# Finished byte addresses instead of element offsets in the table that places each matmul's output in PSUM

## The chip, the cores and the metric

The kernel runs on one core of one Trainium2 chip. The metric is the device time of one execution in microseconds (us).

## The reference, cut to what matters

```python
N, E, D = 4096, 262144, 256
def reference(nodes, edges_src, edges_dst, w_msg, w_self):
    self_out = nodes @ w_self
    msg = nodes[edges_src] @ w_msg
    agg = np.zeros((N, D), dtype=np.float32)
    np.add.at(agg, edges_dst, msg)
    return self_out + agg
```

Every edge adds the transformed row of its source node to its destination node.

## The kernel before

The kernel has two phases. First VectorE sorts all edges by (block of 512 destinations, block of 128 sources, destination). Then the chunk loop turns the sorted edges into counts: 128 edges make one chunk, 2048 chunks in all. For each chunk, two one-hot matrices (source within its block of 128, destination within a window of `W` = 96) are multiplied, and the 128x96 product is added into a ring of six banks, as the kernel's parts of 512 columns are called here, in PSUM (the memory that the kernel takes for the results of its matmuls). *Where* in the ring depends on the data, so the offset comes from a table made after the sort, and TensorE reads it into registers.

The table before holds offsets in elements:

```python
    tt(out=dl[:], in0=dl[:], in1=ex[:], op=ALU.subtract)
    tt(out=poff[:], in0=wr[:], in1=dl[:], op=ALU.add)            # element offset in the ring
    nc.scalar.dma_start(pd[0, :].rearrange("(p g) -> p g", g=G16), poff[:])
    nc.scalar.dma_start(poffs[:], pd[0:1, :])
```

One-hots are built on VectorE for 16 chunks at a time (`SL = 16`). The pair "c" is for chunks; the pair "h" is for heads, the 256 matmuls that open a run at a fixed address:

```python
    def onehots(src, rel, tag):
        for nm, val, wid in (("e", src, P), ("d", rel, W)):
            o = ohp.tile([P, SL // 2, wid, 2], BF16, name=nm + "_oh", tag=nm + tag,
                         bufs=8 if tag == "c" else 2)
            tt(out=o[:], in0=val..., in1=jrow..., op=ALU.is_equal)
```

The loop (cut; "run" is one ring bank of 512 columns, some 8 chunks):

```python
        for c in range(NCOL):                                  # 2048 chunks
            ci = c % SL
            if ci == 0:
                e, d = onehots(slo_b[:, sl_], rel_b[:, sl_], "c")
                # ... and now and then heads[nhead] = onehots(hsl, hrel, "h")
            # ... head_mm(r, ...) where run r starts: fixed address
            if c % 8 == 0:
                regs = [nc.tensor.alloc_register(f"po{c}_{i}") for i in range(8)]
                nc.tensor.load(regs, poffs[0:1, c:c + 8])      # 8 offsets, one load
            off = nc.tensor.snap(regs[c % 8], donate=True, min_val=0, max_val=RING * SEGW - W)
            count_mm(ring[:, bass.ds(off, W)], e, d, ci, False)
            # ... evac(run): ScalarE copies a finished bank to SBUF as bf16 ("at")
            # ... apply_run(run): 4 matmuls out_ps += at.T @ Y (Y: the transformed rows, nodes @ w_msg);
            #     at every 32nd run also 8 "self" matmuls (nodes @ w_self)
```

The matmul is given a byte address, so `off` becomes `off * 4 + 0x2000000`: one fused register operation (for the multiply and the add) for each chunk. The trace before holds 2048 of them on TensorE, of 37 ns each. "TensorE's sequencer" (PEq in the profiles) is the name here for what spends its time on such register operations and on the loads of registers.

## Time and profile before

| | before |
|---|---|
| median of the runs | 985.86 us (985.71 to 986.1) |
| sort and set-up, to the first matmul of the loop | 547.4 us |
| chunk loop | 429.5 us, 256 groups of 8 chunks |
| VectorE busy in the loop | 293 us |

The first excerpt is the page's strip of busy tenths, one digit for each fortieth of the span. VectorE fills the first half. In the loop TensorE shows 8 or 9 tenths.

```profile
PE   0033301131111120302011689888898888898896
...
DVE  3999999989999989898995996776766767767740
```

The second is the windows view of the loop: after the stretch and its length come the busy times (and counts) of PE (TensorE's matmuls), PEld (its weight loads), DVE (VectorE), ACT (ScalarE) and POOL (GpSimd), then the granted clock of TensorE, the DMA share and GB/s.

```profile
547.40:976.90 429.50, 382.12 (x3392) 293.56 (x3392) 292.99 (x285) 156.53 (x270) 0.00 (x0) 0.99 0.03 10
```

PE busy for 382 of 429.5 us looks like a full array. It isn't: the records of matmuls overlap (a ring matmul records some 203 ns, and two can start 42 ns apart, as shown below), so PE also looks busy when they start 115 ns apart. The timeline of two groups shows the pace (start, length, engine, line, operation, count, and in brackets the idle time before it with what ended it):

```profile
703.58 1.01 PE L321 MATMUL ring<-d_oh,e_oh 128*128 128x96 bf16 x9 [0.17 <-issue]
703.58 0.79 PEld L321 LDWEIGHTS <-e_oh 128*128 128x128 bf16 x8 [0.35 <-issue]
...
704.42 0.60 PE L363 MATMUL out_ps<-Y,at 128*128 128x256 bf16 x4
704.62 1.23 DVE L305 TENSOR_TENSOR e_oh<-slo_b,jrow 128x2048 bf16<-128x2048 bf16 x1 [1.16 <-PE ring L321]
...
705.20 1.01 PE L321 MATMUL ring<-d_oh,e_oh 128*128 128x96 bf16 x9 [0.17 <-issue]
```

A group of 8 chunks and one head (9 ring matmuls) starts every 1.62 us. VectorE waits 1.16 us for TensorE before it may overwrite a one-hot. TensorE waits for nothing that the profile names ("issue"). Over the whole loop, the view of waits (total us, times, longest) says the same:

```profile
DVE e_oh L305 <- PE ring L321: 110.6, 96, 1.9
PEld L321 <- issue: 98.8, 269, 5.0
PE ring L321 <- issue: 50.0, 242, 4.7
...
PE ring L321 <- DVE d_oh L305: 0.9, 3, 0.6
```

The page leaves register instructions out, but the trace holds a record of each. Here are single records of TensorE (ns from the start of the span, length in ns; weight loads left out), the end of one group and the start of the next:

```
702443   37  register operation (fused: multiply, add)
702530  203  matmul, ring
702558   37  register operation
702572  204  matmul, ring (head, fixed address)
702645  204  matmul, ring
702673   37  register operation
702760  203  matmul, ring
702798  591  load of 8 registers
702802  270  matmul, out_ps          ... and three more
703489   37  register operation
703575  203  matmul, ring
```

Register operations start 115 ns apart (1630 of 2047 gaps are exactly that). The head slips in 42 ns after its neighbour without delaying anything, so the array could go far faster. What fills the 115 ns can't be read from these records: 37 ns are recorded, 78 ns aren't.

### The profile page before, as it was taken

Reading aid. Unit: us, or ns where it says so; the run is one execution under the profiler, and the core shown is the slowest. Engines: PE = TensorE matmul, PEld = TensorE weight load, DVE = VectorE, ACT = ScalarE, POOL = GpSimd, SP = SyncE. Lnnn points to the kernel's source line nnn. Section 1 sums busy time; section 2 is a strip of 40 time slices with the busy share of each in tenths; the row PEclk is TensorE's granted clock in tenths of the full one; section 3 lists DMA queues with packets and bytes.
Section 4 is the critical chain, followed back from the end, with each engine's and each line's share of the span. In section 5 each row is a group of like instructions: output and inputs, shape, how many; then the busy total and the mean of one; then the engine's idle time right before and its main releaser. Section 6 shows DMA issues by size and latency. Waiting matters only on the chain.

```text
span 983.7 us, 11709 instructions
## 1 busy us (share of the span) xinstructions
PE 477.3 (49%) x3730; PEld 349.9 (36%) x3730; DVE 780.3 (79%) x850; ACT 221.1 (22%) x449; POOL 14.2 (1%) x24
## 2 busy tenths in 40 slices
PE   0033301131111120302011689888898888898896
PEld 0000001121111110202011466666666666676664
DVE  3999999989999989898995996776766767767740
ACT  0011101021010110101003133333333333333333
POOL 4000000000000000000000000000000000000000
PEclk9999999756555555555555699999999999999999
DMA  8611100000000000000003000000000000000000
GB/s 228 134 26 27 24 0 0 1 1 0 0 0 0 0 1 0 0 0 0 0 0 93 1 2 23 1 23 1 1 23 2 23 1 23 2 23 1 23 2 24
DMA packets 25217, 18.03 MB, mean 18 GB/s; under 512 B 11557, under 2 KB 24358, under 8 KB 24390
## 3 DMA queue, kind: packets, MB, share of 16 engines
q1 hardware_dynamic: 19862, 11.59, 4.0%
q0 software_dynamic: 4720, 2.49, 1.9%
q10 hardware_dynamic: 578, 3.16, 0.8%
q8 instruction: 39, 0.64, 0.3%
q14 instruction: 18, 0.15, 0.0%
HBM read 10.12 MB, written 7.37 MB: 18 GB/s over the span
## 4 chain that ended last, share of the span: by engine, by line
DVE 48%; PE 43%; issue 6%; DMA 3%; ACT 0%; DVEq 0%; SPq 0%
PE ring L321 25%; PE out_ps L363 11%; DVE XA_85 L572 7%; DVE XA_84 L572 7%; DVE XA_85 L573 7%; DVE XA_84 L573 6%; DVE XB_86 L572 4%; DVE XB_87 L572 4%; DVE XB_87 L573 3%; DVE XB_86 L573 3%; PE tp_sw L533 3%; DMA XB_86<-in_edges_dst_dram 2%; DVE e_oh L305 1%; DVE d_oh L305 1%; DMA fd<-bcol 1%
## 5 line engine op out<-in xcount | busy, mean ns | idle before, releaser
L321 PE MATMUL ring<-d_oh,e_oh 128*128 128x96 bf16 x2304 | 262.8, 206 | 52.1 <-issue 50.0
L321 PEld LDWEIGHTS <-e_oh 128*128 128x128 bf16 x2304 | 202.6, 97 | 128.1 <-issue 98.8
L305 DVE TENSOR_TENSOR e_oh<-slo_b,jrow 128x2048 bf16<-128x2048 bf16 x128 | 156.4, 1222 | 110.6 <-PE ring L321 110.6
L337 ACT CAST at<-ring 128x512 bf16<-128x512 f32 x256 | 149.8, 586 | 284.2 <-PE ring L321 284.2
L363 PE MATMUL out_ps<-Y,at 128*128 128x256 bf16 x1024 | 153.6, 273 | 0.0
L305 DVE TENSOR_TENSOR d_oh<-rel_b,jrow 128x1536 bf16<-128x1536 bf16 x128 | 121.4, 949 | 0.0
L363 PEld LDWEIGHTS <-at 128*128 128x128 bf16 x1024 | 84.7, 97 | 11.5 <-ACT at L337 0.2
L533 PE MATMUL tp_sw<-ident,XA_85 128*128 128x128 f32 x80 | 20.4, 432 | 111.5 <-DVE XA_85 L573 110.8
L182 PE MATMUL y_ps<-wcat,XT 128*128 128x256 bf16 x64 | 25.2, 394 | 97.3 <-DMA XT<-nodes_bf_dram 97.2
L572 DVE TENSOR_TENSOR XA_85<-XA_84 128x1024 f32<-128x1024 f32 x56 | 68.6, 1225 | 2.2
L572 DVE TENSOR_TENSOR XA_84<-XA_85 128x1024 f32<-128x1024 f32 x55 | 67.4, 1225 | 2.2
L573 DVE TENSOR_TENSOR XA_85<-XA_84 128x1024 f32<-128x1024 f32 x56 | 68.2, 1218 | 0.0
L573 DVE TENSOR_TENSOR XA_84<-XA_85 128x1024 f32<-128x1024 f32 x55 | 67.0, 1218 | 0.0
L533 PEld LDWEIGHTS tp_sw<-ident,XA_85 128*128 128x128 f32 x80 | 14.2, 191 | 117.6 <-DVE XA_85 L573 70.0
L533 PE MATMUL tp_sw<-ident,XA_84 128*128 128x128 f32 x64 | 15.8, 430 | 68.9 <-DVE XA_84 L573 68.9
L182 PEld LDWEIGHTS <-XT 128*128 128x128 bf16 x64 | 6.6, 104 | 115.6 <-DMA XT<-nodes_bf_dram 115.6
L524 ACT COPY XB_86<-tp_sw 128x128 f32<-128x128 f32 x40 | 15.0, 375 | 118.0 <-PE tp_sw L533 97.7
L572 DVE TENSOR_TENSOR XB_86<-XB_87 128x1024 f32<-128x1024 f32 x30 | 36.7, 1225 | 1.0
L572 DVE TENSOR_TENSOR XB_87<-XB_86 128x1024 f32<-128x1024 f32 x30 | 36.7, 1225 | 1.0
L533 PEld LDWEIGHTS tp_sw<-ident,XA_84 128*128 128x128 f32 x64 | 11.5, 190 | 73.3 <-DVE XA_84 L573 70.0
L573 DVE TENSOR_TENSOR XB_87<-XB_86 128x1024 f32<-128x1024 f32 x30 | 36.5, 1218 | 0.0
L573 DVE TENSOR_TENSOR XB_86<-XB_87 128x1024 f32<-128x1024 f32 x30 | 36.5, 1218 | 0.0
(477 smaller groups left out, 286.3 us busy)
## 6 DMA issues: line engine op xcount, KB each, us to landing
out_dram<-o_sb SPq DMA_DIRECT2D x16, 256.0 KB, 2.4
XB_86<-in_edges_dst_dram SPq DMA_DIRECT2D x2, 1024.0 KB, 8.4
XB_87<-in_edges_src_dram ACTq DMA_DIRECT2D x2, 1024.0 KB, 8.5
nodes_bf<-in_nodes_dram POOLq DMA_DIRECT2D x1, 2048.0 KB, 19.9
nodes_bf_dram<-nodes_bf SPq DMA_DIRECT2D x1, 2048.0 KB, 8.7
XT<-nodes_bf_dram SPq DMA_TRANSPOSE x64, 2.4
xs_dram<-XA_85 ACTq DMA_DIRECT2D x1, 1024.0 KB
gball<-gd SPq DMA_DIRECT2D x1, 1024.0 KB, 4.7
```

The source lines that it names most:

```text
L182: nc.tensor.matmul(out=y_ps[:], lhsT=XT[:, k, t * P:(t + 1) * P], rhs=wcat[:, 2 + k, :], start=(k == 0), stop=(k == 1),)
L305: tt(out=o[:], in0=val.rearrange("p (g i) -> p g i", i=2).unsqueeze(2).to_broadcast(shp), in1=jrow[:, 0:wid, :].unsqueeze(1).to_broadcast( ...
L321: mm = nc.tensor.matmul(out=ap, lhsT=e[:, ci // 2, :, ci % 2], rhs=d[:, ci // 2, :, ci % 2], start=start, stop=True, skip_group_check=True ...
L337: ins = nc.scalar.copy(out=at[:], in_=ring[:, b:b + SEGW]).ins
L363: nc.tensor.matmul(out=out_ps[:, t, :], lhsT=at[:, t * P:(t + 1) * P], rhs=Y[:, b, :], start=False, stop=(b == T - 1), skip_group_check=True,)
L524: nc.scalar.copy(out=out_ap, in_=in_ap)
L533: nc.tensor.transpose(tp[:], src[:, g * P:(g + 1) * P], ident[:])
L572: nc.vector.tensor_tensor(out=lo_d, in0=lo_s, in1=hi_s, op=ALU.min)
L573: nc.vector.tensor_tensor(out=hi_d, in0=lo_s, in1=hi_s, op=ALU.max)
```

## The change

Its intent: let VectorE put finished byte addresses into the table, once, so that TensorE's sequencer computes nothing for each chunk.

```diff
+PSUM0 = 0x2000000
@@
     tt(out=poff[:], in0=wr[:], in1=dl[:], op=ALU.add)
+    nc.vector.tensor_scalar(
+        out=poff[:], in0=poff[:], scalar1=2, scalar2=PSUM0,
+        op0=ALU.logical_shift_left, op1=ALU.bitwise_or,
+    )
@@
-            off = nc.tensor.snap(
-                regs[c % 8], donate=True, min_val=0, max_val=RING * SEGW - W
-            )
+            addr = nc.tensor.snap(
+                regs[c % 8], donate=True, min_val=PSUM0, max_val=PSUM0 + 4 * (RING * SEGW - W)
+            ).with_bounds(
+                min_val=PSUM0, max_val=PSUM0 + 4 * (RING * SEGW - W),
+                guaranteed_mod_val=0, out_of_modulus=4,
+            )
+            off = (addr - PSUM0) // 4
             count_mm(ring[:, bass.ds(off, W)], e, d, ci, False)
```

The edit tells the compiler that the address is a multiple of 4, so that it may cancel `(addr - PSUM0) // 4` against `* 4 + PSUM0`.

## The prediction

> **What bounds the kernel now.** The span is 983.7 us. Until 547 us VectorE sorts (the page's slices: DVE 9 tenths); the change leaves that alone but for one tiny operation. From 547 to 977 us runs the chunk loop: 256 groups of 8 chunks. The timeline shows each group as 9 ring matmuls in 1.01 us, 4 out matmuls in 0.44 us and some 0.18 us of "issue". PE's busy share there (89%, the windows view) hides that the array is not the limit. The trace's single records of TensorE show it:
> - every chunk has one fused register operation (2048, 37 ns each, not counted by the page); consecutive ones mostly start exactly 115 ns apart;
> - a head matmul with a fixed address falls 42 to 45 ns after its neighbour and costs nothing: both intervals add up to 115 again. So the array could go at about 43 ns; the 115 ns is the sequencer's;
> - once per group, a load of 8 registers takes 590 ns, and the next register operation starts 100 ns later. From a group's last dynamic matmul to the next group's first is 820 ns; the 4 out matmuls hide inside.
>
> 7 x 115 + 820 = 1625 ns; quiet groups measure 1617 to 1635, the mean is 1671. TensorE's sequencer bounds the loop.
>
> **What the change does.** Each register operation multiplies by 4 and adds 0x2000000, where the ring starts. With finished addresses the expression should collapse to the loaded register, so all 2048 vanish. Register loads, matmuls and one-hots stay. Added: one 128x16 VectorE operation (under 0.3 us).
>
> **What it is worth.** At least the recorded 37 ns. [...]
>
> **Next limit.** VectorE's one-hots: saturated, an e/d pair starts every 2.0 us; 144 pairs make 288 us, 1.13 us per group. The new sequencer period is about 1.26 us, so VectorE, 8 buffers ahead, should rarely be waited for, but its idle time nearly vanishes. ScalarE (0.59 us per group) and the array (0.82 us) are no limit.
>
> **Prediction.** 883 us, 8 in 10 within 864 to 906. Faster by over 2%: 0.93; within 2%: 0.06; slower: 0.01.
>
> **What would show it.** No fused register operations in the loop; dynamic matmuls about 64 ns apart (58 to 75); ring x9 in 0.6 us; "issue" before it still near 0.15 us; register load still 590 ns; mean group near 1.26 us, the loop about 323 us; all before 547 us within 1 us of before; VectorE busy near 90% in the loop.
>
> **What would make it wrong.** (1) The expression doesn't collapse: same time. (2) Only the recorded 37 ns are saved: 908 us. (3) A matmul addressed by a register costs more[...]: nearer 905. (4) VectorE or evacuations bind first: the loop stays over 300 us with such waits in the chain. (5) The register load or its gap grows.

Terms of the sum under "What it is worth" are cut, because no trace of this case showed what they rested on. The sum came to 103 us (986 - 103 = 883 us): 104 us for 2048 operations at 51 ns each (my estimate, with a range of 40 to 57 ns), with 1 to 2 us more and small new waits against them. The 64 ns between matmuls (115 - 51) and the 1.26 us of a group (1671 - 8 x 51 ns) follow from the same estimate.

## The result, and the profile after

The changed kernel takes 842.91 us (842.41 to 843.85, 4 runs) against 985.86 us. The ratio is 0.8551, with a 95% interval of 0.8536 to 0.8566. (Ratios in this document are the mean time of a kernel's fast runs over that of the kernel before in the same rounds, so not quite the ratio of the medians.) That is 143 us less, where 103 were predicted; the time lies below the predicted range.

All of it lies in the loop. The first loop matmul starts at 546.9 us (547.4 before); the added VectorE operation takes 153 ns. The loop takes 287.6 us instead of 429.5:

```profile
546.90:834.50 287.60, 242.18 (x3392) 211.46 (x3392) 284.43 (x285) 156.71 (x270) 0.00 (x0) 0.98 0.04 15
```

The busy time of VectorE, 284.43 of 287.60 us, is now 99% of the loop. The strip shows it too:

```profile
PE   0033320111111111111101112088888888888786
...
DVE  3999999999999999999999998599999999999995
```

The trace has no register operation of TensorE in the loop any more. The timeline of a stretch where one-hots lay ready:

```profile
699.76 0.51 PEld L326 LDWEIGHTS <-e_oh 128*128 128x128 bf16 x9
699.87 0.55 PE L326 MATMUL ring<-d_oh,e_oh 128*128 128x96 bf16 x9
700.12 0.94 DVE L310 TENSOR_TENSOR d_oh<-rel_b,jrow 128x1536 bf16<-128x1536 bf16 x1
...
700.26 0.60 PE L368 MATMUL out_ps<-Y,at 128*128 128x256 bf16 x4
...
700.70 0.55 PE L326 MATMUL ring<-d_oh,e_oh 128*128 128x96 bf16 x9
700.99 1.21 DVE L310 TENSOR_TENSOR e_oh<-slo_b,jrow 128x2048 bf16<-128x2048 bf16 x1
```

A group now starts every 0.83 us, and PE has no gap. In the single records the ring matmuls follow each other by 43 to 45 ns. The register load still takes 588 ns, but in this stretch it starts at the fourth or so ring matmul of the group *before* the one that it serves; it has gone behind the array's work.

In most places one-hots are not ready, and then TensorE waits for VectorE:

```profile
690.10 0.94 DVE L310 TENSOR_TENSOR d_oh<-rel_b,jrow 128x1536 bf16<-128x1536 bf16 x1
...
691.09 0.55 PE L326 MATMUL ring<-d_oh,e_oh 128*128 128x96 bf16 x9 [0.37 <-DVE d_oh L310]
...
692.10 0.94 DVE L310 TENSOR_TENSOR d_oh<-rel_b,jrow 128x1536 bf16<-128x1536 bf16 x1
...
693.10 0.55 PE L326 MATMUL ring<-d_oh,e_oh 128*128 128x96 bf16 x9 [0.18 <-DVE d_oh L310]
```

The waits of the loop have turned round. The 110.6 us in which VectorE waited for TensorE are gone from the list, and the weight loads' "issue" has fallen from 98.8 to 43.2 us; new are the waits of matmuls and weight loads for one-hots:

```profile
PEld L326 <- issue: 43.2, 96, 0.8
PE ring L326 <- DVE d_oh L310: 38.4, 88, 1.6
PEld L326 <- DVE e_oh L310: 11.7, 15, 0.9
...
PE ring L326 <- issue: 5.5, 3, 4.6
```

The mean group is 1116 ns (1671 before); 555 ns x 256 groups = 142 us, which is the whole gain. VectorE starts one pair every 2.005 us, and 144 pairs x 2.005 / 256 groups = 1.128 us per group, about 12 ns from the measured mean.

So the new limit is plain. What the trace alone does not say is why the old one gave way so completely. The prediction had the sequencer go on at some 64 ns per chunk.

### The profile page after: what moved, and what is told of

It reads as the page before. It is cut to its first block, busy times and chain, and to the rows that moved or that the text cites. A ratio compares the mean times of both kernels' runs of the same rounds, so it can differ in the third digit from the quotient of the medians.

```text
span 841.4 us, 9662 instructions
## 1 busy us (share of the span) xinstructions
PE 337.7 (40%) x3730; PEld 268.0 (32%) x3730; DVE 772.9 (92%) x851; ACT 221.6 (26%) x449; POOL 15.1 (2%) x24
## 5 line engine op out<-in xcount | busy, mean ns | idle before, releaser
L326 PE MATMUL ring<-d_oh,e_oh 128*128 128x96 bf16 x2304 | 147.5, 208 | 44.6 <-DVE d_oh L310 38.4
L310 DVE TENSOR_TENSOR e_oh<-slo_b,jrow 128x2048 bf16<-128x2048 bf16 x128 | 154.3, 1206 | 0.0
L326 PEld LDWEIGHTS <-e_oh 128*128 128x128 bf16 x2304 | 132.2, 99 | 66.6 <-issue 48.1
L368 PEld LDWEIGHTS <-at 128*128 128x128 bf16 x1024 | 86.5, 97 | 7.4 <-ACT at L342 0.6
L542 PE MATMUL tp_sw<-ident,XA_85 128*128 128x128 f32 x80 | 20.5, 436 | 111.3 <-DVE XA_85 L582 110.6
L542 PEld LDWEIGHTS tp_sw<-ident,XA_85 128*128 128x128 f32 x80 | 14.3, 193 | 117.4 <-DVE XA_85 L582 70.1
L187 ACT CAST Y<-y_ps 128x256 bf16<-128x256 f32 x32 | 11.9, 372 | 96.8 <-PE y_ps L183 96.8
```

Source lines behind the costliest of these rows:

```text
L187: nc.scalar.copy(out=Y[:, t, :], in_=y_ps[:])
L310: tt(out=o[:], in0=val.rearrange("p (g i) -> p g i", i=2).unsqueeze(2).to_broadcast(shp), in1=jrow[:, 0:wid, :].unsqueeze(1).to_broadcast( ...
L326: mm = nc.tensor.matmul(out=ap, lhsT=e[:, ci // 2, :, ci % 2], rhs=d[:, ci // 2, :, ci % 2], start=start, stop=True, skip_group_check=True ...
L368: nc.tensor.matmul(out=out_ps[:, t, :], lhsT=at[:, t * P:(t + 1) * P], rhs=Y[:, b, :], start=False, stop=(b == T - 1), skip_group_check=True,)
L542: nc.tensor.transpose(tp[:], src[:, g * P:(g + 1) * P], ident[:])
```

## The experiments

Two questions: what did the 115 ns per chunk consist of, and what binds now?

Theory P, formed on seeing the result: a register operation has a fixed price of about 115 ns on TensorE's sequencer, of which the trace records 37; a matmul whose address comes from a register costs the sequencer almost nothing. Its rivals are in the expectations: A (the price is the arithmetic), W (the matmul waits for a freshly written register), S (the price is paid for each change between register operation and matmul). The prediction's own split, an estimated 51 ns for the operation and the other 64 of the 115 ns for the matmul, is the fourth.

The OR with 0x2000000 leaves a finished address as it is, so these kernels stay correct.

### One register operation per chunk put back

```diff
+            fin = nc.tensor.alloc_register(f"fin{c}")
+            nc.tensor.reg_alu(fin, regs[c % 8], PSUM0, ALU.bitwise_or)
             addr = nc.tensor.snap(
-                regs[c % 8], donate=True, ...
+                fin, donate=True, ...
```

> After, with one register operation per chunk put back (an OR with 0x2000000, which leaves a finished address as it is); the matmul reads its result. One plain operation instead of the fused multiply and add of before. Theory P (fixed price): a register operation costs TensorE's sequencer about 115 ns[...]: group period back near 1625 to 1670 ns, about 986 us [...]. Rival A (arithmetic): the cost grows with the number of operations fused, so one costs about half: about 57 ns per chunk, loop near the one-hots' limit, 845 to 870 us.

Measured: 980.58 us, ratio to before 0.9954 (0.9926 to 0.9983), correct. The operations record 32 ns (37 for the fused two) and start 112 or 113 ns apart; a quiet group takes 1598 ns. So one OR takes back nearly all that the change had gained (138 of 143 us). Theory A falls: two operations fused cost 115 ns, one costs 112.5.

### The same operation, its result read 8 chunks later

```diff
             if c % 8 == 0 and c + 8 < NCOL:
+                regs = ...                      # one group ahead
+                nc.tensor.load(regs, poffs[0:1, c + 8:c + 16])
+            nxt = nc.tensor.alloc_register(f"fin{c + 8}")
+            nc.tensor.reg_alu(nxt, regs[c % 8], PSUM0, ALU.bitwise_or)
+            fins.append(nxt)
             addr = nc.tensor.snap(
-                regs[c % 8], ...
+                fins[c], ...
```

> The same OR per chunk at the same place in the stream, but its result is read by the matmul 8 chunks later (registers are loaded one group ahead). Theory P (fixed price per register operation, whoever reads it): same as e1, about 986 us, operations 115 ns apart. Rival W (the matmul waits for a register that has just been written): the operations no longer hold anything up, dynamic matmuls go at about 43 to 60 ns, 843 to 850 us.

Measured: 979.99 us, ratio 0.9948 (0.992 to 0.9977), correct; operations again 112 or 113 ns apart. Who reads the result, and when, does not matter: theory W falls.

### The operation on every second chunk

```diff
+            fin = regs[c % 8]
+            if c % 2 == 1:
+                fin = nc.tensor.alloc_register(f"fin{c}")
+                nc.tensor.reg_alu(fin, regs[c % 8], PSUM0, ALU.bitwise_or)
```

> The OR only on odd chunks, 4 per group. Theory P: the sequencer's group is 700 + 4 x 115 = 1160 ns in quiet groups, about 1200 in the mean, a little over the 1125 ns of the one-hots: 855 to 880 us. Were the slow pace a mode of the whole group (any register operation makes all register-addressed matmuls slow), it would stay near 986 us.

Measured: 868.17 us, ratio 0.8813 (0.8788 to 0.8839), correct. A quiet group takes 1137 ns, 461 less than with eight operations: 115 each. The price is paid per operation; it is no mode of the whole group.

### The eight operations of a group in a row

```diff
                 nc.tensor.load(regs, poffs[0:1, c:c + 8])
+                for i in range(8):
+                    nc.tensor.reg_alu(fins[i], regs[i], PSUM0, ALU.bitwise_or)
             addr = nc.tensor.snap(
-                regs[c % 8], ...
+                fins[c % 8], ...
```

> The 8 ORs of a group in a row directly after the register load, then the 8 matmuls. Theory P: 8 x 115 ns in a row, then the matmuls at 43 ns; the sequencer's group is 1620 to 1670 ns as before, about 986 us. Rival S (the unrecorded 78 ns is paid when the stream changes from a register operation to a matmul and back, not per operation): 8 operations follow each other at 40 to 60 ns, plus one change: group about 700 + 450 = 1150 ns, 850 to 870 us.

Measured: 962.83 us, ratio 0.9774 (0.9746 to 0.9803), correct. Between the two expectations, and much nearer to P. The single records (ns, length) show why:

```
701265  592  load of 8 registers
701961   32  register operation
702054   32  register operation      ... eight of them, 92 or 93 ns apart
702609   32  register operation
702669  206  matmul, ring
702711  213  matmul, ring
702761  590  load of 8 registers
```

In a row, with nothing between them, the operations still start 92.5 ns apart while each records 32. So about 60 ns of every operation are its own and unrecorded, and some 20 ns more appear when a matmul stands between two of them. S is right for those 20 ns and wrong for the rest. The parts of a quiet group are 590 (load) + 105 (to the first operation) + 7 x 92.5 + 152 (last operation to next load) = 1494 ns; the median group takes 1537. Without its eight operations the quiet group leaves 1494 - 8 x 92.5 = 754 ns, 56 more than the 698 of the other runs (below). Those 56 ns are paid once per group; for what, no run shows.

### Half of the one-hots, after the change

```diff
             if ci == 0:
-                e, d = onehots(slo_b[:, sl_], rel_b[:, sl_], "c")
+                if (c // SL) % 2 == 0:
+                    e, d = onehots(slo_b[:, sl_], rel_b[:, sl_], "c")
```

> After, with each pair of chunk one-hots built once and used for two blocks of 16 chunks (wrong result on purpose): VectorE's work in the loop falls from 144 pairs to 80, 160 us. Theory D (after is bound by VectorE's one-hots, 2.0 us per pair): the loop shortens to the next limit, the array at 9 x 43 + 4 x 109 = 823 ns per group plus the 8 self matmuls every 32 groups, about 218 us: 775 us (768 to 790). Rival: the after loop is bound by TensorE (its sequencer or the array): no change, 843 us.

Measured: 799.2 us, ratio 0.8099 (0.8064 to 0.8134); the result is wrong on purpose. The direction is as theory D has it: VectorE's busy time falls from 284 to 156 us, and the kernel gets 44 us faster. So VectorE's work does bind the kernel after. The size missed: 799 is above the 768 to 790 expected. Quiet groups have the array's pace (median 830 ns against 823 expected), but the mean is 941. The waits of the loop (window 560 to 770 us) name what is left:

```profile
DVE e_oh L310 <- PE ring L326: 60.9, 13, 5.9
...
PE ring L326 <- issue: 6.6, 13, 1.2
```

The page's groups put all of those 60.9 us before the one-hots of the heads:

```profile
L310 DVE TENSOR_TENSOR e_oh<-hsl,jrow 128x2048 bf16<-128x2048 bf16 x16 | 19.5, 1221 | 60.9 <-PE ring L326 60.9
```

VectorE waits there until TensorE has used an older pair of the heads, for example 3.13 us until the operation that starts at 693.04 us. At 695.32 us TensorE in its turn has waited 0.70 us; the profile calls it "issue", and it ends 0.19 us after the head's one-hots are finished, so it was probably for them. That the two buffers of the heads cause this was not tested.

### Half of the one-hots, before the change

The same edit on the kernel before.

> Before, with the same halving of the one-hots (wrong result on purpose). If before was bound by TensorE's sequencer alone, nothing changes but small waits: 975 to 985 us. If VectorE was part of the limit of before, it falls by 20 us or more.

Measured: 985.42 us, ratio 0.9986 (0.9946 to 1.0026). VectorE has half the work in the loop, and the time stays:

```profile
547.00:977.00 430.00, 383.06 (x3392) 293.81 (x3392) 158.15 (x158) 156.78 (x270) 0.00 (x0) 0.99 0.03 10
```

The mean group takes 1670 ns as before. So VectorE was no part of the limit before. Nor was the array: after the change the same matmuls follow each other by 43 to 45 ns. What is left is TensorE's sequencer.

### The register load twice

```diff
                 nc.tensor.load(regs, poffs[0:1, c:c + 8])
+                regs2 = [nc.tensor.alloc_register(f"pq{c}_{i}") for i in range(8)]
+                nc.tensor.load(regs2, poffs[0:1, c:c + 8])
+                regs = regs[0:4] + regs2[4:8]
```

> After, with the 8 registers of each group loaded by two loads (the first half of the matmuls reads one set, the second half the other). Theory: the sequencer's only remaining cost in after is the load, 590 ns plus about 100 not recorded, 700 ns per group, hidden under the one-hots' 1125 ns. With two, 1380 ns per group come to the front: loop about 355 us, 905 us (890 to 925). Were loads free to overlap with each other, the array or the one-hots, 843 us.

Measured: 931.82 us, ratio 0.9443 (0.9406 to 0.9481), correct. The sequencer binds again:

```profile
PEld L326 <- issue: 148.1, 233, 0.8
PE ring L326 <- issue: 89.4, 208, 0.6
DVE e_oh L310 <- PE ring L326: 63.3, 78, 1.9
```

The median group is 1394 ns (1380 expected). The time is 7 us above the expected range because the mean group is 1465: I had left out the longer groups that the kernel before has as well (1671 in the mean against 1617 to 1635 in quiet ones).

This run also holds the most telling pair of numbers. From the first load of a group to the second, with nothing between them, the median is 688 ns, of which 587 are recorded. From the second load to the next group's first, with 8 register-addressed matmuls, 5 fixed ones and 13 weight loads between, it is 707 ns. So 26 engine instructions add 19 ns to the sequencer's time. A matmul addressed by a register does not cost it the 64 ns that the prediction left for it: eight of those would have added 512 ns.

### A version that goes with the new limit

Since VectorE binds now, larger one-hots should help if part of each of its operations is fixed, as the two sizes suggest (see the expectation; the kernel after measures 1135 and 869 ns from start to start for 2048 and 1536 elements, which leaves an estimated 4 x 869 - 3 x 1135 = 71 ns if the rest grows with the size):

```diff
-SL = 16
+SL = 32
@@
-                bufs=8 if tag == "c" else 2,
+                bufs=4 if tag == "c" else 2,
```

> After, with one-hots built for 32 chunks at a time instead of 16 (4 buffers instead of 8, same values). If VectorE binds the loop and about 65 ns of each of its 288 operations is fixed (1130 and 870 ns from start to start for 2048 and 1536 elements in the same lanes: 0.55 and 0.57 ns per element), half of that, 9 us, falls away, less some 3 us for a later first block and a longer last one: 835 to 839 us, inside 2%. Were TensorE the limit, 843 us or a little more.

Measured: 833.91 us, ratio to before 0.8447 (0.8421 to 0.8474), correct: 1 us below the expected range. A one-hot of twice the size starts its successor after 2202 and 1669 ns, against 2 x 1135 and 2 x 869, so 68 and 69 ns of each operation are fixed (65 expected). It ran again beside the kernel after and a mixed version (blocks of 32, but 16 for the first two, the last two and the heads):

> The kernel after, unchanged, as the measure on this chip for the two below: 842 to 844 us.

> One-hots for 32 chunks at a time, unchanged from c1: 833 to 835 us, 1.1% faster than after.

> As c1, but the first two and the last two blocks, and the heads' one-hots, are of 16 chunks. VectorE's fixed part rises by 1 us for the heads and 0.5 us for the small blocks; the first matmul should come some 3 us earlier than in c1 and the last matmuls some 1.5 us sooner after the last one-hot: 830 to 833 us. If start and tail do not count, 835 us.

On that chip the kernel after took 843.0 us (842.87 to 843.31), blocks of 32 took 833.25 us (832.46 to 835.25), and the mixed version took 835.94 us (835.04 to 837.73), all correct. Blocks of 32 take 1.2% less than the kernel after, and their runs lie clear of its runs; against the mixed version the ranges just overlap. From the heads' one-hots that open the loop (at 544 us) to the end of the last one-hot, VectorE takes 275.3 us with them, 286.7 in the kernel after, and 278.2 in the mixed version. So the mixed version's earlier start did not pay for its smaller operations: that expectation was missed, and only about half of the 2.9 us follows from its ten extra pairs. In the groups of the repeated run, VectorE has no idle time before the one-hots of the chunks:

```profile
L310 DVE TENSOR_TENSOR e_oh<-slo_b,jrow 128x4096 bf16<-128x4096 bf16 x64 | 145.5, 2273 | 0.0
...
L310 DVE TENSOR_TENSOR d_oh<-rel_b,jrow 128x3072 bf16<-128x3072 bf16 x64 | 111.4, 1741 | 0.0
```

## Why the prediction was wrong

- **What bounds before: right.** Halving VectorE's work left before at 985.4 us; putting one OR back per chunk brought after to 980.6 us.
- **What vanishes: right.** All 2048 register operations are gone, and the start of the loop moved by 0.5 us only.
- **What it is worth: this step failed.** The prediction put the operation at 51 ns (40 to 57) of the 115 and left 64 for the matmul. The operation measured 112 to 115 ns between matmuls, more than double. The split was my estimate; no trace showed it. The trace already spoke against it: a head matmul with its weight load cost the 115 ns nothing (it starts 42 to 45 ns after its neighbour, and the operations around it stay 115 ns apart). I took the matmul with a register address for an exception, without saying so. It isn't one: 26 engine instructions, eight of them such matmuls, add 19 ns.
- **The group's sum, corrected.** The sequencer's group is about 698 ns for load and rest, plus 112 to 115 ns for each register operation: 1598 - 8 x 112.5 = 698 with the OR, 1617 - 8 x 115 = 697 before. With four operations that gives 1148 to 1158 (1137 measured). With none it gives 698, and the catching-up groups at the start of the loop after measured 696 and 703.
- **The 820 ns at the border of groups: wrong to carry over.** The prediction let it shrink by one register operation only. With the load starting during the matmuls of the group before, as the trace after shows it, all 698 ns are hidden, and "issue" before the group all but disappeared (5.5 us in 3 places of the loop, where it was 50.0 us in 242) instead of staying near 0.15 us.
- **Next limit: the number was right, its place was not.** The one-hots were put at 288 us for the loop and were expected to be "rarely waited for". The loop took 287.6 us. Since the sequencer fell to 698 ns and not to 1260 ns per group, VectorE's 1125 ns became the limit, and halving its work showed it. The list of what would make the prediction wrong names this limit too, in (4), but only as a reason for a slower result. With the estimated 40 to 57 ns for each operation the sequencer's group came to 1671 - 8 x 57 = 1215 ns at the least, above VectorE's 1125, so the predicted range never reached this limit.
- **Signs.** Ring matmuls 43 to 45 ns apart (64 predicted), mean group 1.116 us (1.26), VectorE busy 99% of the loop (90%): these missed. Nine ring matmuls in 0.55 us (0.6) and the load at 588 ns (590) held.

What stays open: what the sequencer does in the 60 to 80 ns of a register operation that no record shows, and why some groups are longer (before, every seventh or eighth takes 1745 ns, where quiet ones take 1617 to 1635). The prediction's further 1 to 2 us was not shown: the kernel after is bound by VectorE.

## What to carry to other kernels

Price a register operation by the distance between starts, not by its recorded length: here 32 to 37 ns recorded stood for 92 to 115 ns, while engine instructions beside it were almost free (26 of them added 19 ns). If a cost can be moved into data (a table of finished addresses, made here by one VectorE operation of 153 ns), move it, even if it is a single OR: here one OR for each chunk cost 138 us. And when a limit may fall further than assumed, compute the next limit's floor and give it a place in the range: here it was the answer.
